# One pooled projection moved ahead of V, and products with V that move their operand in alternation

## The chip, the cores and the metric

The kernel runs on one core of a Trainium2 chip. A core has a matrix engine (TensorE, PE in the profile, with PEld for its weight loads), a vector engine (VectorE, DVE), a scalar engine (ScalarE, ACT), GpSimd (POOL) and a queue engine (SyncE, SP) that here issues most DMAs. Each has its own queue of instructions, which it works through in order; semaphores tie the queues together. Matrix products read SBUF and add into PSUM, which has eight banks of 128 partitions by 512 float32 values here.

The metric is the device time of one execution in microseconds (us), taken as the median of several runs.

## The reference

One layer of a streaming encoder over 512 tokens of width 1024, in float32: a half-weighted feed-forward, a mixer, a second half-weighted feed-forward, and a final norm.

```python
x = x + 0.5 * swiglu_ffn(rmsnorm(x, g1), w_gate1, w_up1, w_down1)
x = x + hybrid_mixer(rmsnorm(x, g), w_in, q_gain, k_gain, rel_bias, pool_w, pool_scale, w_out)
x = x + 0.5 * swiglu_ffn(rmsnorm(x, g2), w_gate2, w_up2, w_down2)
x = rmsnorm(x, g_final)
```

The mixer projects its input to q, k, v and u, each 512 wide. With q, k and v it computes chunked attention for 8 heads of 64 (each query sees its own chunk of 64 tokens and the 8 before it, with a relative-position bias; q and k are normed per head). With u it computes, in four groups of 128 channels, the trailing mean over 2, 4, 8 or 16 tokens less the token itself, then a 128 by 128 map and a scale. Both results are put side by side and go through one output projection.

```python
proj = h @ w_in                       # q | k | v | u
a = chunked_attention(q, k, v, ...)   # softmax(q k / 8 + bias) v, by head
p = multiscale_pool(u, pool_w, pool_scale)
return concat([a, p]) @ w_out
```

## The kernel before

**Precision by threes.** A float32 operand is split into a high part (rounded, made by ACT) and a low part (the remainder, made by DVE). A product is three matmuls: high with high, high with low, low with high. The function `mm3` writes them at lines 198 to 200, so three rows L198, L199, L200 are one "triple" over one block of 128 by 128 weights and 512 (sometimes 256) columns. `mm3` views the moving operand as two halves and moves a column of the first, then one of the second, in alternation; the result then stands in PSUM in that mixed order, and whoever takes it out reads PSUM with a stride of two (`ordered`) and writes in natural order (`natural`).

**Stages.** The first feed-forward, the mixer (about 310 to 496 us of the span) and the second feed-forward follow each other; only the mixer is changed.

**The mixer's order is planned.** Every piece of work is a `job` with an engine, a cost, a rank and the jobs that it waits for. `plan` walks through time with these costs, lets each engine take the ready job with the lowest rank for which there are buffers (eight PSUM banks, three places for split weights, two for raw weights and so on), and that sequence is written out for PE, DVE, ACT and POOL word for word. On the chip the engines keep to it, whatever the real durations are. Projections and the output projection are fillers: PE takes them when nothing of the attention is ready.

**The projections.** `ORDER` lists them: the query-key columns of heads 0 to 3 (`0`), V, the query-key columns of heads 4 to 7 (`1`), and the four pooled groups (`"u"`, the one with window 16 first). Each query-key half and V takes four weight blocks of 1024 columns, each pooled group takes one, that is 8 triples. SP loads raw blocks, ACT splits off the high part (L1117), DVE the low part (L1122). POOL also issues DMAs that add up weights for the second feed-forward (L717), tied to split blocks 12 to 19.

**A pooled group** after its projection: DVE scales it (L1422), POOL makes window sums (L1430, one to four steps), DVE forms the difference (L1438, and L1443 and L1444 for the first tokens), ACT and DVE split it (L1447, L1450), PE maps it (a triple that reads `wp`), ACT and DVE split the mapped result (L1263, L1267).

**A head**: scores (L1516, two heads at a time), bias and maximum on DVE (L1524), exponential on ACT (L1532), reciprocal (L1540), normalization on ACT (L1543), transposes on PE (L1580), the transposed probabilities split by ACT (L1589, high) and DVE (L1594, low) in three groups, then the product with V: eight matmuls at L1605, stationary the four blocks of V (with high and low side by side, so that one product gives two results of 64 rows), moving the probabilities' high and low parts. The keys are in four blocks of 128; block `j` moves only columns from `j * 128` on, so the eight are of 512, 512, 384, 384, 128, 128, 256 and 256 columns. ACT takes out the high half (L1612), DVE the rest (L1615) and the sum with the low half (L1621).

**The output projection** begins with the first four blocks of output rows, over the attention's heads 0 to 3, the pooled groups, and heads 4 to 7 in that order; the other blocks may begin after head 7's product.

Of the kernel before, what the change touches and what calls it, by code (L numbers as in the profile page):

```python
# [8 lines left out]
F32 = mybir.dt.float32  # L9
# [3 lines left out]
ALU = mybir.AluOpType  # L13
# [3 lines left out]
P = 128  # L17
# [3 lines left out]
NT = S // P  # L21
# [4 lines left out]
HD = 64  # L26
# [14 lines left out]
LATE = 12  # L41


ORDER = (0, "v", 1, "u", "u", "u", "u")
RANK = dict(
    weights=(-1.0, 0.905, 3.0), qk=2.0, turn=1.015, head=0.9, pool=0.965, map=3.0, u=0.99,
    score=0.99, evac=0.3, bias=1.2, wp=1.5, add=0.935, next=0.965,
# [9 lines left out]
def layer(  # L57
# [31 lines left out]
    nc = tc.nc  # L89
# [851 lines left out]
    with tc.tile_pool(name="mix", bufs=1, reuse_waits="tile") as mpool:  # L941
# [30 lines left out]
        def in_mix(tag, n, dtype, bufs, many=1):  # L972
            def make(slot):
                z = [
                    mpool.tile([P, n], dtype, tag=f"{tag}{i}", name=name(tag), bufs=bufs)
                    for i in range(many)
                ]
                return z if many > 1 else z[0]

            return bufs, make  # L980

        def part_at(slot):
# [10 lines left out]
            u=in_mix("u", PAD + S, F32, 1),  # L993
# [5 lines left out]
        buf = {}  # L999
# [84 lines left out]
        begins = []  # L1084
        for what in ORDER:
            begins.append(len(sources))
            if what == "v":
                sources += [wV[kp] for kp in KPS]
            elif what == "u":
                sources.append(wU[3 - sum(z == "u" for z in ORDER[: len(begins) - 1])])  # L1090
            else:
# [35 lines left out]
        for i in range(len(sources)):  # L1127
            z = job("sp", 0.4, i, load_raw(i), gets=[("raw", ("raw", i))], lag=2.0 if i < RAW else 3.6)
# [12 lines left out]
        for k, t in enumerate((7.2, 8.5, 9.7, 12.8)):  # L1141
            z = job("sp", 0.0, -9, None, lag=t)
# [46 lines left out]
        z = job("act", 1.8, -1, root_of, [z])  # L1189
        at_r = job("dve", 0.8, -1, reciprocal_root, [z], uses=["total"])  # L1190
        z = job("dve", 0.65, -1, diagonal, [at_r], [("t", "diag")])
        z = job("pe", 0.9, -1, spread, [z], [("bank", "wide")], ["diag"])
# [62 lines left out]
        z = job("sp", 0.4, 5, lambda: nc.sync.dma_start(buf["wp"], wP), gets=[("t", "wp")], lag=3.6)  # L1255
        z = job("act", 0.6, RANK["wp"], pool_weights(0), [z, ready[3]])
# [49 lines left out]
        v, at_v = [None] * NT, [None] * NT  # L1306
# [175 lines left out]
        n_u, n_before = 0, len(jobs)  # L1482
        for what, first in zip(ORDER, begins):
            if what == "u":
# [84 lines left out]
        def head(h):  # L1569
            rank = RANK["head"] + 0.01 * h - 0.001  # L1570
            rows = slice((h % 2) * HD, (h % 2 + 1) * HD)
            spots = {}
            pair = [("aT", h // 2, n) for n in range(2)]
# [14 lines left out]
            def high(group, n):  # L1588
                return lambda: nc.scalar.copy(buf["pT", h, group][0], buf["tp", h, group][:, :n])  # L1589
# [8 lines left out]
                return emit  # L1598

            def multiply():  # L1600
                o = buf["o", h]
                for j in (0, 1, 3, 2):
                    group, at = spots[j]
                    for i in range(2):
                        nc.tensor.matmul(  # L1605
                            o[:, j * P :], v[j][:, h, :, :],
                            buf["pT", h, group][i][:, at : at + (NT - j) * P],
                            start=j == 0 and i == 0, stop=j == 2 and i == 1,
                        )

            def out_high():
                nc.scalar.copy(buf[pair[0]][rows, :], buf["o", h][:HD, :])  # L1612

            def out_rest():
                nc.vector.tensor_tensor(  # L1615
                    buf["rest", h][rows, :], buf["o", h][:HD, :],
                    buf[pair[0]][rows, :].bitcast(F32), op=ALU.subtract,
                )

            def out_low():  # L1620
                nc.vector.tensor_tensor(  # L1621
                    buf[pair[1]][rows, :], buf["rest", h][rows, :], buf["o", h][HD:, :], op=ALU.add
                )

            lows = []
            for group in GROUPS:
                n = 0
                for j in group:
                    spots[j] = group, n
                    n += (NT - j) * P  # L1630
                z = at_turn[h, group] = job(
                    "pe", 0.03 + n / P * 0.109, rank, turned(group),
                    [at_prob[h, t] for t in range(min(group), NT)] + [at_turn.get((h - 1, group))],
                    [("bank", ("tp", h, group))], [("p", h, t) for t in range(min(group), NT)],
                )
                z = job(
                    "act", 0.13 + n * 0.00082, rank, high(group, n), [z],
                    [("wide" if n == S else "slim", ("pT", h, group))],
                )
                lows.append(  # L1640
                    job("dve", 0.08 + n * 0.00106, rank, low(group, n), [z], uses=[("tp", h, group)])
                )
            z = at_product[h] = job(
                "pe", 1.28, rank, multiply, lows + at_v, [("bank", ("o", h))],
                [("pT", h, group) for group in GROUPS],
            )
            z = job("act", 0.53, rank, out_high, [z], [("m", key) for key in pair])
            z = job("dve", 0.62, rank, out_rest, [z], [("t", ("rest", h))])
# [60 lines left out]
        for ds, chunks in (((0, 1, 2, 3), FOUR), ((4, 5), (0, 1)), ((6, 7), (0, 1))):  # L1709
            units = {d: [] for d in ds}  # L1710
            for chunk in chunks:
                if len(ds) == 4:
                    part, k0 = chunk
                    i = first_out + FOUR.index(chunk)
                    items = [(part, k, d) for k in ((k0, k0 + 1) if part else (k0 + 1, k0)) for d in ds]
                else:
                    part, k0 = chunk, 0
                    i = first_out + ds[0] + part
# [13 lines left out]
            for d in ds:  # L1732
                z = job("dve", 0.65, RANK["add"], add_out(d), units[d], uses=[("out", d)])
# [30 lines left out]
    with tc.tile_pool(name="act2", bufs=1, reuse_waits="tile") as apool, ExitStack() as in_order:  # L1764
# [86 lines left out]
        for tt in range(2):  # L1851
            scaled(u2[tt], p1[tt][0][0], 0.5, u2[tt], ALU.subtract)
            residual(1, 2 + tt, p5[tt][0][0])
            for i in (2 + tt, NT + tt, NT + 2 + tt):
                op = ALU.subtract if i < NT + 2 else ALU.add
                z = natural(xt[i])
# [45 lines left out]
        with tc.manual_schedule(engines={E.PE, E.DVE, E.Activation, E.Pool}):  # L1902
            last_product(0, p7[0][0])
            settle(0, two, 0, 0, S)
            v = mean(two, [1])
            r = inverse(v)
            v = small.tile([P, 1], F32, tag="rc", name=name("v"), bufs=8)
# [9 lines left out]
            v = more(v, 0)  # L1917
            root = small.tile([P, 1], F32, tag="rc", name=name("root"), bufs=8)
            nc.scalar.activation(root, ssq[:, three, 2:3], AF.Sqrt, scale=1.0 / D, bias=v)
            u = more(v, 2)  # L1920
# [94 lines left out]
```

## Time and profile before

| what | value |
|---|---|
| time, median of 3 runs | 811.85 us (811.62 to 812.27) |
| the profiled execution's own time | 811.69 us |
| its span, first to last instruction | 809.7 us |
| granted TensorE clock | 0.997 |
| PE busy | 797.8 us, 99% |
| DVE, ACT, POOL busy | 712.8, 498.8, 147.2 us |
| PE idle by its waits in the mixer | 0.6 us for L1621, 0.3 us for L1594 |

In the profile a row names the engine, the line of the program, the instruction and the tiles: `mm` and `a` are PSUM banks, `m` split parts, `parts` split weights, `pTw` and `pTs` transposed probabilities, `v` the blocks of V. PE's instructions are pipelined: a matmul's time reaches past the start of the next, so the pace is read from starts, not from durations.

### The profile page before, as it was taken

The page shows a single profiled execution, that of the slowest core. Times are in us where ns is not written, and L with a number is a line of the kernel's source. Part 1 is how long each engine was busy: PE and PEld are TensorE (multiplying, and loading weights), DVE is VectorE, ACT ScalarE, POOL GpSimd, SP SyncE. Part 2 cuts the span into 40 slices and gives each one's busy share as a digit, 9 for nine tenths or more (in the row PEclk, how much of TensorE's full clock was granted, in tenths as well). Part 3 has the DMA queues.
Part 4 walks back from the last instruction along what each step waited for, and adds up shares of the span by engine and source line. Part 5 has one row for each costly group of instructions (what it writes and reads, how often), then busy time and mean ns, then how long its engine had stood idle before and what let it go on. Part 6 is the DMA issues. An engine that isn't in the chain of part 4 may idle for free.

```text
span 809.7 us, 14959 instructions
## 1 busy us (share of the span) xinstructions
PE 797.8 (99%) x5730; PEld 749.1 (93%) x5730; DVE 712.8 (88%) x1133; ACT 498.8 (62%) x854; POOL 147.2 (18%) x234
## 2 busy tenths in 40 slices
PE   9999999999999999999999999999999999999995
PEld 8889999999999999888888888899999999988985
DVE  7899999999996997778688788999999999987996
ACT  8446655556666665659659545465666655765683
POOL 0022212223220000100256354111111011100010
PEclk9999999999999999999999999999999999999998
DMA  8276889979999774431599777256666566969642
GB/s 289 76 208 208 237 226 247 216 189 249 248 292 316 220 219 147 142 124 34 156 258 248 196 198 210 80 112 204 172 184 151 163 185 168 272 210 344 211 120 104
DMA packets 73703, 158.56 MB, mean 196 GB/s; under 512 B 6544, under 2 KB 31648, under 8 KB 73248
## 3 DMA queue, kind: packets, MB, share of 16 engines
q1 hardware_dynamic: 49664, 109.09, 40.0%
q0 software_dynamic: 23680, 48.24, 28.3%
q8 instruction: 45, 0.74, 0.4%
q10 hardware_dynamic: 288, 0.27, 0.1%
q14 instruction: 26, 0.21, 0.1%
HBM read 153.38 MB, written 50.34 MB: 252 GB/s over the span
## 4 chain that ended last, share of the span: by engine, by line
PE 91%; DVE 4%; ACT 1%; issue 1%; DVEq 0%; ACTq 0%
PE mm L198 19%; PE mm L200 19%; PE mm L199 19%; PE a L199 10%; PE a L200 9%; PE a L198 9%; PE mm L1605 1%; PE mm L1516 1%; DVE aside L365 1%; PE a L1580 1%; PE mm L1580 1%; DVE aside L371 0%; PE a L1516 0%; DVE parts L133 0%; PE a L1605 0%
## 5 line engine op out<-in xcount | busy, mean ns | idle before, releaser
L571 ACT ACTIVATE t<-mm 128x256 f32<-128x256 f32 x105 | 40.5, 386 | 110.8 <-PE mm L200 108.8
L132 ACT CAST parts<-raw 128x1024 fp32r<-128x1024 f32 (+2 forms) x77 | 74.1, 968 | 54.7 <-PE mm L199 20.5
L133 DVE TENSOR_TENSOR parts<-raw,parts 128x1024 fp32r<-128x1024 f32 (+2 forms) x77 | 85.8, 1121 | 15.1 <-ACT parts L132 14.7
L199 PE MATMUL mm<-ha,parts 128*128 128x256 f32 x280 | 77.0, 275 | 0.0
L200 PE MATMUL mm<-ha,parts 128*128 128x256 f32 x280 | 77.0, 275 | 0.0
L198 PE MATMUL mm<-ha,parts 128*128 128x256 f32 x280 | 77.0, 275 | 0.0
L715 POOL COPY mark<-t 128x1 f32<-128x1 f32 x40 | 15.9, 397 | 330.9 <-DVE t L615 244.8
L717 POOL DMA_DIRECT2D wsum<-in_wB_dram x72 | 71.1, 1123 | 26.1 <-DMA wsum<-wsum 14.1
L482 DVE TENSOR_TENSOR parts<-wsum,parts 128x1024 fp32r<-128x1024 f32 x53 | 64.5, 1217 | 5.1 <-ACT parts L477 5.1
L477 ACT CAST parts<-wsum 128x1024 fp32r<-128x1024 f32 x53 | 53.9, 1047 | 0.6 <-PE mm L200 0.3
L198 PEld LDWEIGHTS mm<-ha,parts 128*128 128x128 f32 x280 | 53.8, 192 | 0.1
L199 PEld LDWEIGHTS mm<-ha,parts 128*128 128x128 f32 x280 | 53.8, 192 | 0.1
L200 PEld LDWEIGHTS mm<-ha,parts 128*128 128x128 f32 x280 | 53.8, 192 | 0.0
L198 PE MATMUL mm<-hhi,parts 128*128 128x512 f32 x128 | 49.6, 391 | 0.2
L200 PE MATMUL mm<-hhi,parts 128*128 128x512 f32 x128 | 48.7, 384 | 0.8 <-DVE parts L133 0.8
L133 DVE TENSOR_TENSOR ah<-acts,ah 128x512 fp32r<-128x512 f32 (+1 forms) x72 | 47.1, 662 | 2.7 <-ACT ah L132 2.4
L199 PE MATMUL mm<-hlo,parts 128*128 128x512 f32 x128 | 48.4, 379 | 0.0
L132 ACT CAST ah<-acts 128x512 fp32r<-128x512 f32 (+1 forms) x72 | 40.9, 580 | 8.8 <-PE mm L199 6.4
L482 DVE TENSOR_TENSOR parts<-raw,parts 128x512 fp32r<-128x512 f32 (+1 forms) x52 | 43.6, 858 | 0.5 <-ACT parts L477 0.5
L500 DVE TENSOR_TENSOR wsum<-raw 128x1024 f32<-128x1024 f32 x35 | 42.6, 1217 | 0.0
L477 ACT CAST parts<-raw 128x512 fp32r<-128x512 f32 (+1 forms) x52 | 39.2, 755 | 4.7 <-DMA raw<-in_wA_dram 3.4
L1122 DVE TENSOR_TENSOR parts<-raw,parts 128x1024 fp32r<-128x1024 f32 x24 | 30.1, 1258 | 11.6 <-ACT parts L1117 11.5
(342 smaller groups left out, 3062.0 us busy)
## 6 DMA issues: line engine op xcount, KB each, us to landing
raw<-in_wA_dram SPq DMA_DIRECT2D x87, 512.0 KB, 4.7
wsum<-in_wB_dram POOLq DMA_DIRECT2D x60, 512.0 KB, 7.5
raw<-wsum SPq DMA_DIRECT2D x36, 512.0 KB, 4.6
raw<-in_wB_dram SPq DMA_DIRECT2D x30, 512.0 KB, 4.9
wsum<-wsum POOLq DMA_DIRECT2D x20, 512.0 KB, 5.0
x<-in_xT_dram SPq DMA_DIRECT2D x16, 256.0 KB, 6.1
raw<-in_wQK_dram SPq DMA_DIRECT2D x8, 512.0 KB, 3.6
wsum<-in_wB_dram POOLq DMA_DIRECT2D x12, 256.0 KB, 5.5
```

What stands on the lines that cost most here:

```text
L132: nc.scalar.copy(hi, src)
L133: nc.vector.tensor_tensor(lo, src, hi.bitcast(F32), op=ALU.subtract)
L198: nc.tensor.matmul(acc, a[0], high, start=start, stop=False, **more)
L199: nc.tensor.matmul(acc, a[0], low, start=False, stop=False, **more)
L200: nc.tensor.matmul(acc, a[1], high, start=False, stop=stop, **more)
L477: nc.scalar.copy(hi, src)
L482: nc.vector.tensor_tensor(lo, src, hi.bitcast(F32), op=ALU.subtract)
L500: nc.vector.tensor_tensor(z, raw[:, : 2 * S], raw[:, S : 3 * S], op=ALU.add)
L571: nc.scalar.activation(natural(dst), ordered(src), AF.Copy, scale=scale)
L717: nc.gpsimd.dma_start(self.rows(i, g), self.rows(self.terms[i][at], g), **(dict(accum_op=ALU.add) if at else {}),)
L1122: nc.vector.tensor_tensor(lo, buf["raw", i], hi.bitcast(F32), op=ALU.subtract)
L1580: nc.tensor.transpose(buf["tp", h, group][:, n : n + P], buf["p", h, t][:, j * P : (j + 1) * P], ident,)
```

## The change

Two things, both in the mixer.

```diff
-ORDER = (0, "v", 1, "u", "u", "u", "u")
+ORDER = (0, "u", "v", 1, "u", "u", "u")
@@ head: products with V
             def multiply():
-                o = buf["o", h]
+                o = buf["o", h].rearrange("p (b i a) -> p b i a", a=2, i=P // 2)
                 for j in (0, 1, 3, 2):
                     group, at = spots[j]
                     for i in range(2):
+                        turned = buf["pT", h, group][i][:, at : at + (NT - j) * P]
                         nc.tensor.matmul(
-                            o[:, j * P :], v[j][:, h, :, :],
-                            buf["pT", h, group][i][:, at : at + (NT - j) * P],
+                            o[:, j:], v[j][:, h, :, :],
+                            turned.rearrange("p (b a i) -> p b i a", a=2, i=P // 2),
                             start=j == 0 and i == 0, stop=j == 2 and i == 1,
                         )
 
+            def result(half):
+                o = buf["o", h][half * HD : (half + 1) * HD, :]
+                return o.rearrange("p (b i a) -> p b a i", a=2, i=P // 2)
+
+            def by_block(z):
+                return z[rows, :].rearrange("p (b a i) -> p b a i", a=2, i=P // 2)
+
             def out_high():
-                nc.scalar.copy(buf[pair[0]][rows, :], buf["o", h][:HD, :])
+                nc.scalar.copy(by_block(buf[pair[0]]), result(0))
```

`out_rest` and `out_low` change their operands in the same way.

**The order.** The pooled group with window 16 is projected between the first query-key half and V. It is no more than an entry moved in a tuple, but the planner makes a new sequence for the whole mixer out of it.

**The alternation.** Within each block of 128 columns the products with V now move a column of the first 64 and one of the second 64 in turn. The result stands in that order in its bank, and the three instructions that take it out read it with a stride of two and write natural order. The number of instructions and their sizes are the same.

Lines after the change are 1 to 8 higher from there on: the product is L1606, its evacuation L1620, L1623 and L1629.

On PE, at the end of the first query-key half (`mm_4306` is its last bank), before:

```order
L200 MATMUL mm_4306<-parts,hlo_4256 128x512
L198 MATMUL a_4469<-parts,hhi_4121 128x512
L199 MATMUL a_4469<-parts,hhi_4121 128x512
L200 MATMUL a_4469<-parts,hlo_4122 128x512
L198 MATMUL a_4475<-parts,hhi_4121 128x512
```

and now:

```order
L200 MATMUL mm_4306<-parts,hlo_4256 128x512
L198 MATMUL a_4469<-hhi_4234,parts 128x512
L199 MATMUL a_4469<-hlo_4235,parts 128x512
L200 MATMUL a_4469<-hhi_4234,parts 128x512
L198 MATMUL a_4469<-hhi_4241,parts 128x512
```

Behind the arrow the moving operand stands first. Where V's triples began (they move the split weights past the tokens, in four banks), the pooled group's eight triples stand now (they move the tokens past the split weights, all into one bank), and V's follow.

On PE, ahead of head 6's product (its bank is `a_5717` before and `mm_5764` after), before:

```order
L198 MATMUL mm_5683<-m_5604,wp_4378 128x512
L199 MATMUL mm_5683<-m_5605,wp_4378 128x512
L200 MATMUL mm_5683<-m_5604,wp_4379 128x512
L198 MATMUL mm_5697<-m_5611,wp_4378 128x512
L199 MATMUL mm_5697<-m_5612,wp_4378 128x512
L200 MATMUL mm_5697<-m_5611,wp_4379 128x512
L1580 MATMUL a_5705<-ident,prob_804_5510 128x128
L1580 MATMUL a_5705<-ident,prob_799_5486 128x128
L1605 MATMUL a_5717<-pTw_5691,v_4748 128x512
```

and now:

```order
L198 MATMUL a_5752<-m_5711,wp_4378 128x512
L199 MATMUL a_5752<-m_5712,wp_4378 128x512
L200 MATMUL a_5752<-m_5711,wp_4379 128x512
L198 MATMUL a_5665<-m_5674,parts 128x512
L199 MATMUL a_5665<-m_5675,parts 128x512
L200 MATMUL a_5665<-m_5674,parts 128x512
L1606 MATMUL mm_5764<-pTw_5727,v_4827 128x512
L1606 MATMUL mm_5764<-pTw_5728,v_4827 128x512
```

Two maps and a pair of transposes for head 7 stood right ahead of it; now one map and a triple of the output projection stand there, and between the products of heads 5 and 6 there are seven triples where there were three.

On ACT, the last instructions ahead of head 7's probability copies (L1589 into `pTw`), before:

```order
L1543 ACTIVATE prob_809_5538<-prob_809_5538,sm_5487 128x256
L1117 CAST parts<-raw_5345 128x1024
L1612 CAST m_5735<-a_5717 64x512
L1447 CAST m_5742<-t_5709 128x512
L1589 CAST pTw_5750<-mm_5730 128x512
```

and now:

```order
L1117 CAST parts<-raw_5533 128x1024
L1620 CAST m_5790<-mm_5764 64x512
L1589 CAST pTs_5797<-mm_5784 128x256
L1543 ACTIVATE prob_825_5594<-prob_825_5594,sm_5546 128x128
L1543 ACTIVATE prob_826_5598<-prob_826_5598,sm_5546 128x256
L1117 CAST parts<-raw_5656 128x1024
L228 ACT_TABLE_LOAD
L228 ACTIVATE table<-ones 128x1
L1589 CAST pTw_5841<-a_5822 128x512
```

Two normalizations of head 7 (L1543), a second weight split and the table load now stand between head 6's result and these copies, where a pooled difference (L1447) stood.

More of the change, by code (lines that the diff above doesn't have):

```diff
@@ L1604, in multiply @@
                     for i in range(2):
+                        turned = buf["pT", h, group][i][:, at : at + (NT - j) * P]
                         nc.tensor.matmul(
-                            o[:, j * P :], v[j][:, h, :, :],
-                            buf["pT", h, group][i][:, at : at + (NT - j) * P],
+                            o[:, j:], v[j][:, h, :, :],
+                            turned.rearrange("p (b a i) -> p b i a", a=2, i=P // 2),
                             start=j == 0 and i == 0, stop=j == 2 and i == 1,
                         )
+            def result(half):
[3 more added lines that the diff above has]
+                return z[rows, :].rearrange("p (b a i) -> p b a i", a=2, i=P // 2)
             def out_high():
-                nc.scalar.copy(buf[pair[0]][rows, :], buf["o", h][:HD, :])
+                nc.scalar.copy(by_block(buf[pair[0]]), result(0))
             def out_rest():
                 nc.vector.tensor_tensor(
-                    buf["rest", h][rows, :], buf["o", h][:HD, :],
-                    buf[pair[0]][rows, :].bitcast(F32), op=ALU.subtract,
+                    by_block(buf["rest", h]), result(0), by_block(buf[pair[0]].bitcast(F32)),
+                    op=ALU.subtract,
                 )
@@ L1621, in out_low @@
                 nc.vector.tensor_tensor(
-                    buf[pair[1]][rows, :], buf["rest", h][rows, :], buf["o", h][HD:, :], op=ALU.add
+                    by_block(buf[pair[1]]), by_block(buf["rest", h]), result(1), op=ALU.add
                 )
```

## The prediction

> **What bounds the kernel now.** I read the page's engine totals and its chain first, then the stretch of the mixer in which the change works.
>
> ```profile
> PE 797.8 (99%) x5730; PEld 749.1 (93%) x5730; DVE 712.8 (88%) x1133; ACT 498.8 (62%) x854; POOL 147.2 (18%) x234
> PE 91%; DVE 4%; ACT 1%; issue 1%; DVEq 0%; ACTq 0%
> ```
>
> TensorE is busy for 99% of the span, and the chain that ended last runs over PE for 91%. So what counts is the time that PE spends per matmul and the few places where it waits. The totals hide the second, so I asked for the busy time from the second half's scores to head 4's product with V, and from there to head 7's (columns: window, PE, weight loads, DVE, ACT, POOL, clock, DMA share, GB/s).
>
> ```profile
> 420.00:433.30 13.30, 13.30 (x95) 11.32 (x95) 12.10 (x47) 11.09 (x34) 11.66 (x14) 1.00 0.99 249
> 433.30:454.40 21.10, 20.09 (x110) 16.93 (x109) 20.02 (x45) 20.23 (x43) 9.95 (x14) 1.00 0.71 176
> ```
>
> The clock is full (1.00). In the second stretch DVE (20.02 of 21.10 us) and ACT (20.23) are as full as PE, and only there does PE stop. Its timeline (start, time, instruction, wait in brackets):
>
> ```profile
> 443.06 0.60 PE L1580 MATMUL a<-ident,prob 128*128 128x128 f32 x4
> 443.72 0.45 PE L198 MATMUL mm<-m,wp 128*128 128x512 f32 x1
> 444.23 0.38 PE L200 MATMUL mm<-m,wp 128*128 128x512 f32 x1
> 445.17 0.45 PE L198 MATMUL mm<-m,wp 128*128 128x512 f32 x1 [0.56 <-DVE m L1621]
> 445.97 0.44 PE L1580 MATMUL a<-ident,prob 128*128 128x128 f32 x2
> 446.73 1.27 PE L1605 MATMUL a<-pTw,v 128*128 128x512 f32 x6 [0.32 <-DVE pTw L1594]
> ```
>
> Starts should follow each other by 0.22 us after a 512-wide matmul and 0.11 per transpose. 443.06 to 443.72 is 0.66 where 0.44 is due (0.2 lost), 444.23 to 445.17 is 0.94 for 0.22 (0.7), 445.97 to 446.73 is 0.76 for 0.27 (0.5); with 0.1 at head 6's first matmul and 0.2 behind its last, **PE loses about 1.8 us here**. The chain of waits says to whom:
>
> ```profile
> 443.61 0.69 DVE t L1615
> 444.32 0.69 DVE m L1621
> 445.47 0.60 DVE m L1450
> 446.07 0.61 DVE pTw L1594
> ```
>
> DVE works without a gap through head 5's result (L1615, L1621), a pooled difference (L1450) and head 6's probabilities (L1594), and PE waits for its queue.
>
> **The change, part by part.** *Alternating moves.* The projections' matmuls already move two halves of their operand alternately; the products with V move straight ahead. Their pace side by side, around head 0's product:
>
> ```profile
> 378.71 0.38 PE L199 MATMUL mm<-parts,hhi 128*128 128x512 f32 x1
> 379.57 0.38 PE L200 MATMUL mm<-parts,hlo 128*128 128x512 f32 x1
> 379.79 1.15 PE L1605 MATMUL mm<-pTw,v 128*128 128x512 f32 x6
> 380.78 0.45 PE L1605 MATMUL mm<-pTs,v 128*128 128x256 f32 x2
> 381.07 0.38 PE L198 MATMUL a<-parts,hhi 128*128 128x512 f32 x1
> ```
>
> Five alternating 512-wide matmuls take 379.79 - 378.71 = 1.08 us, 0.216 each (0.42 ns a column). The eight of a product take 381.07 - 379.79 = 1.28 us. The same eight at the alternating pace: two of 512 at 0.216, two of 384 at 0.162, and four of 128 and 256 columns at 0.109, the pace of narrow alternating matmuls in the feed-forward:
>
> ```profile
> 129.95 0.28 PE L200 MATMUL a<-xa,wlo 128*128 128x256 f32 x1
> 130.50 0.28 PE L199 MATMUL mm<-xa,parts 128*128 128x256 f32 x1
> ```
>
> That is five starts in 0.55 us. The sum is 0.43 + 0.32 + 0.44 = 1.19, so 0.09 less per head and **-0.7 us** for eight heads, all of it on PE. What no row shows is an alternation over 64 columns (256 bytes); the rows have 256 and 128 columns. Bounds: nothing gained, and the full 0.7. I take the full value, since both distances in the trace run at the same pace. A loss is priced under the rivals.
>
> The Trainium skill ("TensorE: Matmul & The Clock Gate", back-to-back issue gap) gives a matmul N/2.4 + 2.5 ns whatever its addresses, 215.8 ns for 512; by it the sum here would be zero. The 1.28 us above stand against it, since its figures would give an estimated 1.09 for the product already now.
>
> *The results of the product.* They now leave PSUM with a stride of two. ACT and DVE pay nothing measurable for that:
>
> ```profile
> L1612 ACT CAST m<-mm x6: 577/578/580, 381.3 to 455.9; 64x512 fp32r<-64x512 f32 x6
> L1312 ACT ACTIVATE t<-mm,r x6: 687/687/688, 342.3 to 405.4; 128x512 f32<-128x512 f32 x6
> L1422 DVE TENSOR_TENSOR u<-mm,rb x2: 671/678/684, 434.2 to 442.9; 128x512 f32<-128x512 f32 x2
> ```
>
> L1422 reads with that stride in 678 ns, where the straight L1615 takes 0.69 us. ACT's strided, scaled L1312 takes 687 ns against 578, at most 0.11 more. I count nothing; without cover it would be 0.1 us on each of two or three heads whose result PE waits for.
>
> *The pooled projection.* Its 24 matmuls keep their time, and so do its weight split, window sums and map: moved, not added. Its weight load passes the four V loads and four query-key loads on SP; on POOL its four window sums go ahead of the weight-sum DMAs instead of between them. Up to the first scores PE has 26 triples (three 512-wide matmuls, 0.65 us) where it had 25, and 28 instead of 17 between the first scores and head 0's product, so the first half gets 7 us more cover for some 4 us of extra ACT and DVE work. I count no wait there.
>
> The scores now fall into eight groups instead of seven. Entering and leaving one costs PE time:
>
> ```profile
> 419.73 0.38 PE L200 MATMUL mm<-hhi,parts 128*128 128x512 f32 x1
> 420.04 0.49 PE L1516 MATMUL mm<-m,m 64*128 64x512 f32 x1
> 420.38 0.39 PE L1516 MATMUL mm<-m,m 64*128 64x512 f32 x1
> 422.17 0.48 PE L198 MATMUL mm<-hhi,parts 128*128 128x512 f32 x1
> 422.49 0.38 PE L199 MATMUL mm<-hlo,parts 128*128 128x512 f32 x1
> ```
>
> 0.31, 0.34 and 0.32 where 0.22 is the pace: **+0.3 us**.
>
> *The late stretch.* Between the products of heads 4 and 7 PE has 25 triples instead of 19, with the same 28 transposes: 21.1 - 1.8 + 3.9 - 0.3 = 22.9 us of its own work. DVE loses one pooled difference with its edge (1.0 like the other pooled steps together), two L1450 (1.2) and one L1422 (0.6), and gains a map's low part (0.7, as L1615) and a weight split (1.2, below): about 19 us. So DVE is no longer the bound, and between heads 5 and 6 stand seven triples instead of three. **The old 1.8 us go.** But ACT gains there, priced by:
>
> ```profile
> L1117 ACT CAST parts<-raw 128x1024 fp32r<-128x1024 f32 x24 | 25.1, 1047 | 19.0 <-PE mm L200 9.2 <-PE a L199 5.8 <-DMA raw<-in_wQK_dram 2.2
> L1532 ACT ACTIVATE prob<-prob,sm 128x512 f32<-128x512 f32 (+3 forms) x32 | 17.7, 556 | 5.0 <-DVE sm L1524 4.9
> L1543 ACT ACTIVATE prob<-prob,sm 128x512 f32<-128x512 f32 (+3 forms) x32 | 16.9, 559 | 0.0
> L228 ACT ACT_TABLE_LOAD x3 | 3.8, 1283 | 0.1
> L1447 ACT CAST m<-t 128x512 fp32r<-128x512 f32 x4 | 2.4, 630 | 0.0
> L1122 DVE TENSOR_TENSOR parts<-raw,parts 128x1024 fp32r<-128x1024 f32 x24 | 30.1, 1258 | 11.6 <-ACT parts L1117 11.5
> ```
>
> One weight split (1.05), one map (0.6), one normalization (0.5) and the table load with its dummy (1.5), less two L1447 (1.1), all a little under their means since neighbours overlap: +2.5 us, about 22 of 22.9. It is full, and unevenly so. From head 6's last probability copy to head 7's last normalization it has twelve instructions: four normalizations, three exponentials, two maps, a weight split, a head's result, a copy: 4 x 0.5 + 1.5 + 2 x 0.6 + 1.0 + 0.5 + 0.35 = 6.5 us, starting about 1 us before head 6's product. PE reaches the transposes for which it needs them after 1.2 + 5 x 0.65 + 0.3 = 4.8 us. **A new wait of about 0.7 us** stands there. Ahead of head 4's product the cover shrinks. Its last operand and its start were:
>
> ```profile
> 431.17 0.68 DVE L1594 TENSOR_TENSOR pTw<-a,pTw 128x512 fp32r<-128x512 f32 x1
> 433.14 1.14 PE L1605 MATMUL a<-pTw,v 128*128 128x512 f32 x6
> ```
>
> That is 433.14 - 431.85 = 1.3 us of slack. Now PE has 9 triples instead of 11 there (1.3 less) while DVE gets a split and an L1450 more and a pooled difference less. The slack is used up, and I put 0.3 there and at head 5. Together +1.0, bounds 0 and 2.5 (both waits at twice the size and the ones of before in part).
>
> **Sum** against the profiled execution's 811.69 us: -0.7 + 0.3 - 1.8 + 1.0 = -1.2, 810.5. The median of the runs is 811.85, 0.16 above the profiled one, so **810.6 us**.
>
> **The rivals.** *The old wait goes and no new one comes* (ACT has its normalizations done in time): -0.7 + 0.3 - 1.8 + 0.2 = -2.0, 809.8. For it: in the stretch ahead ACT had 11.09 of 13.30 us, so it may start earlier. Against it: 22 of 22.9 us.
>
> *Alternation over 64 columns brings nothing*: 811.3.
>
> *The weights come late.* DMA is at 0.99 in the stretch before, and ACT's two splits of output weights now stand ahead of head 7's copies, with everything behind them in one queue. The slowest of such loads:
>
> ```profile
> DMA to landing us min/median/max: 3.3/3.6/7.8
> ```
>
> 4.2 us late, less ACT's 1 us of reserve, puts 3.2 on PE in place of the 0.7: 810.6 + 2.5 = 813.1. It decides once a load lands more than 1 us behind the split's turn.
>
> *Alternation costs.* If two addresses 256 bytes apart disturbed each other, the nearest slow pace is that of the unrounded 512-wide matmuls:
>
> ```profile
> 342.09 1.02 PE L1182 MATMUL a<-t,ones 128*128 128x512 f32 x2
> L1182 PE MATMUL a<-t,ones x2: 593/593/593, 342.1 to 342.5; 128*128 128x512 f32 x2
> ```
>
> 1.02 - 0.593 = 0.43 us apart, twice 0.216. A product of 2560 columns would take 2.14 instead of 1.28 us: +6.9 for eight heads in place of -0.7, 818. It decides the sign once a product costs 0.06 us more than now, which eats the 0.5 us gained elsewhere. The Trainium skill ("SBUF — State Buffer", Door 1: The DMA port swizzle) says that reads that cross to a new 16-byte line each time pay a penalty, which speaks for this; the alternating triples, faster than the straight products, speak against it.
>
> **How the numbers follow.** Forecast 0.45 (810.0 to 811.1), no new wait 0.22, no gain from alternation 0.20, late weights 0.07, costly alternation 0.06. A change under 0.2% (1.6 us, 810.2 to 813.5) can't be told from none. The forecast lies just inside: of its 0.45 I give 0.13 to faster, of the second case 0.21; late weights divide 0.04 slower, 0.03 same. So faster 0.34, same 0.56, slower 0.10. The range leaves out a tenth at each end: 809.3 to 812.4.
>
> **What would show it.** Eight products of 1.19 us, and eight evacuations still near 0.58 us; PE starting its maps on time between heads 5 and 6; a wait of PE for ACT's L1543 ahead of head 7's transposes; at most 0.5 us lost at head 4. Products of 1.28 us would make the first term wrong; waits in the first half or a PE wait behind a weight split would make the others wrong.

## The result and the profile after

The changed kernel takes 819.02 us (median of 6 runs, 816.74 to 821.42) where the kernel before, run beside it, takes 811.94: a ratio of 1.0086 (95% interval 1.0068 to 1.0103). It is slower by 7 us. I had forecast 810.6, in a range that ended at 812.4.

The profiled execution after took 819.33 us, 7.6 more than the one before. First the chain that ended last, from its page:

```profile
PE 81%; DVE 6%; DMA 4%; ACT 2%; issue 2%; POOL 1%; SPq 0%; DVEq 0%; ACTq 0%; POOLq 0%
```

The chain, which ran over PE for 91%, now runs over it for 81% and over DMA for 4%. PE's waits of 0.3 us and more (which line waited for what; us in total, times, longest), without three outside the mixer that the kernel before has too:

```profile
PE a L1516 <- ACT m L1447: 4.8, 1, 4.8
PE mm L1356 <- DVE t L1346: 1.1, 1, 1.1
...
PE a L198 <- ACT t L571: 0.7, 1, 0.7
...
PE a L198 <- DVE m L1629: 0.3, 1, 0.3
```

The first two are new in the mixer. One score group of the second half (L1516) waits 4.8 us, and the transposes of the first query-key half (L1356) wait 1.1 us. L571 lies in the first feed-forward, which the change does not touch. The wait for L1629 stands at 452.8 us, behind head 4's result (452.22 to 452.91 us on VectorE); the wait for head 5's result that I had read in the kernel before is gone.

The chain of waits through the long one, in order of time (start, us, what):

```profile
411.63 8.66 DMA wsum<-in_wB_dram
...
422.76 1.73 POOL wsum L717 x2
424.49 5.91 issue
...
430.95 1.09 POOL us L1430
...
433.25 1.06 POOL us L1430
...
434.34 0.69 DVE t L1438
...
435.35 0.63 ACT m L1447
436.07 0.76 PE a L1516
```

GpSimd issues two weight-sum DMAs (L717). The third of the same step reads a sum that another DMA is still making, so it can be issued only 5.91 us later, as GpSimd's timeline shows as well (start, time, instruction, wait in brackets):

```profile
430.42 0.53 POOL L717 DMA_DIRECT2D wsum<-wsum  x1 [5.93 <-DMA wsum<-in_wB_dram]
```

Behind it in GpSimd's queue stand the window sums (L1430) of the second pooled group, window 8. They end at 434.3 us. VectorE's L1438 waits for them, and ScalarE's L1447 waits for that. VectorE's timeline says what this holds up:

```profile
434.34 0.69 DVE L1438 SCALAR_TENSOR_TENSOR t<-us,u 128x512 f32<-128x512 f32 x1 [6.46 <-POOL us L1430]
...
435.23 0.69 DVE L1524 CUSTOM_DVE_ANT_0 prob<-a,bias 128x512 f32<-128x512 f32 x1
```

and ScalarE's:

```profile
435.35 0.62 ACT L1447 CAST m<-t 128x512 fp32r<-128x512 f32 x1 [7.55 <-DVE t L1444]
435.96 0.72 ACT L1532 ACTIVATE prob<-prob,sm 128x512 f32<-128x512 f32 x1
```

VectorE stands still for 6.46 us and ScalarE for 7.55, each in front of a pooled step, while the score maxima (L1524) and exponentials (L1532) of the third pair of heads stand right behind it. Without the pooled step in front, the first L1524 starts at 429.66 us (experiment 4). PE needs the bank that the first L1524 frees. The waits view names L1447 because its end lies next to PE's start.

Then the clock. The windows around the wait (columns: window, PE, weight loads, DVE, ACT, POOL, granted clock, DMA share, GB/s):

```profile
432.00:434.00 2.00, 0.00 (x0) 0.00 (x0) 0.00 (x0) 0.00 (x0) 1.84 (x3) 0.88 1.26 491
...
438.00:440.00 2.00, 2.00 (x14) 1.88 (x11) 1.84 (x11) 2.00 (x8) 0.00 (x0) 0.50 0.98 172
440.00:442.00 2.00, 2.00 (x12) 1.39 (x12) 1.58 (x10) 1.97 (x6) 0.00 (x0) 0.92 1.08 188
```

In the middle of the stretch the mean is 0.50. If the clock is either full or half, a mean of 0.88 puts the drop at 433.5 us (1.52 us in full and 0.48 by half), 0.92 puts the return at 440.3. (Windows of half a microsecond bear this out: 1.00 up to 433.5, then 0.51 and 0.50, and 0.67 from 440.0 to 440.5 before 1.00.) PE works again from 436.07, so 4.2 us of work ran at half speed, which costs 2.1 us.

The alternation does what it says. Head 0's product on PE's timeline after:

```profile
390.46 1.09 PE L1606 MATMUL mm<-pTw,v 128*128 128x512 f32 x6
391.66 0.38 PE L198 MATMUL a<-parts,hhi 128*128 128x512 f32 x1
```

That is 391.66 - 390.46 = 1.20 us, where it was 1.28.

**The balance** of the two profiled executions: +4.8 (wait) + 2.1 (half clock) + 1.1 (L1356) + 0.3 (the eighth score group, taken from the prediction, not measured by itself) - 0.7 (alternation) - 1.8 (the old late wait) + 0.3 (the wait for L1629) + 1.4 (the mixer starts later, see experiment 9) = 7.5 of 7.6 us.

### The profile page after: what moved, and what is told of

Read it like the earlier page. It is cut to its first block, busy times and chain, and to the rows that moved or that the text cites. A ratio compares the mean times of both kernels' runs of the same rounds, so it can differ in the third digit from the quotient of the medians.

```text
span 817.5 us, 14948 instructions
## 1 busy us (share of the span) xinstructions
PE 799.9 (98%) x5730; PEld 750.7 (92%) x5730; DVE 716.3 (88%) x1133; ACT 499.3 (61%) x854; POOL 148.2 (18%) x234
## 4 chain that ended last, share of the span: by engine, by line
PE 81%; DVE 6%; DMA 4%; ACT 2%; issue 2%; POOL 1%; SPq 0%; DVEq 0%; ACTq 0%; POOLq 0%
PE mm L198 18%; PE mm L200 18%; PE mm L199 18%; PE a L198 8%; PE a L199 8%; PE a L200 8%; DMA wsum<-in_wB_dram 3%; DMA raw<-in_wA_dram 1%; PE mm L1516 1%; DVE t L1346 1%; DVE aside L365 1%; POOL wsum L717 1%; PE mm L1606 0%; DVE aside L371 0%; POOL us L1430 0%
## 5 line engine op out<-in xcount | busy, mean ns | idle before, releaser
L571 ACT ACTIVATE t<-mm 128x256 f32<-128x256 f32 x105 | 40.5, 386 | 110.6 <-PE mm L200 108.3
L717 POOL DMA_DIRECT2D wsum<-in_wB_dram x72 | 71.9, 1153 | 29.5 <-DMA wsum<-wsum 15.8
L1122 DVE TENSOR_TENSOR parts<-raw,parts 128x1024 fp32r<-128x1024 f32 x24 | 31.2, 1299 | 9.7 <-ACT parts L1117 9.7
```

The source lines that it names most:

```text
L571: nc.scalar.activation(natural(dst), ordered(src), AF.Copy, scale=scale)
L717: nc.gpsimd.dma_start(self.rows(i, g), self.rows(self.terms[i][at], g), **(dict(accum_op=ALU.add) if at else {}),)
L1122: nc.vector.tensor_tensor(lo, buf["raw", i], hi.bitcast(F32), op=ALU.subtract)
```

## The experiments

Each kernel was run beside the kernel before on the same chip, whose median was 812.0 to 812.2 us.

**1 and 2. Each half of the change alone.** The first is the changed kernel with the old `ORDER`, so that the alternation stays:

```diff
-ORDER = (0, "u", "v", 1, "u", "u", "u")
+ORDER = (0, "v", 1, "u", "u", "u", "u")
```

> The alternation of the column halves alone, in the order of the kernel before. Theory (the loss belongs to the moved projection): the eight products keep the 1.20 us that the trace after the change shows instead of 1.28, so 0.7 us are gained and the time is 811.2 us, ratio 0.9991, with no new wait on TensorE over 0.5 us in the mixer. Rival (the alternation loses elsewhere, through the evacuations that read and write in strides): part of the 7 us comes with it, 813 us or more.

Measured: 811.42 us against 812.12, ratio 0.9992 (0.9983 to 1.0000). PE's waits in the mixer are those of the kernel before:

```profile
PE mm L198 <- DVE m L1629: 0.6, 1, 0.6
...
PE a L1606 <- DVE pTw L1594: 0.3, 1, 0.3
```

The second kernel is the one before with the new `ORDER` and straight products.

> The moved projection alone, with the products' columns in their old order. Theory: the whole loss is here. The 4.8 us wait at the scores of the second half stands in the trace at about 431 to 436 us, and the time is that of the changed kernel plus the 0.7 us that the alternation gave: 819.7 us, ratio 1.0095. Rival (the strided evacuations hold up VectorE and ScalarE and the order only brings it to light): the wait is gone or under 1 us, and the time is 813 us or less.

Measured: 818.43 us, ratio 1.0077 (1.0063 to 1.0091). The long wait is there, though shorter than expected:

```profile
PE a L1516 <- ACT m L1447: 3.0, 1, 3.0
```

Its windows, with the end of the lowered clock:

```profile
438.00:440.00 2.00, 2.00 (x9) 1.38 (x9) 0.78 (x4) 1.06 (x4) 0.00 (x0) 0.50 1.03 187
440.00:442.00 2.00, 2.00 (x11) 1.65 (x10) 1.99 (x5) 1.07 (x5) 1.47 (x1) 0.92 0.57 104
```

So the order brings the loss, +6.3, and the alternation, -0.7, is no part of it. I had expected 819.7, and the two do not quite add up to the 7.1 of the whole change: 5.6, within the width of the intervals, with a long wait that took 3.0 us in this profile and 4.8 and 4.0 in the two of the changed kernel. The wait is 1.8 us shorter than in the changed kernel, but the time hardly is, because the clock is at half from 433.5 (432 to 434 us has a mean of 0.87) to 440.3 us here too, and all but 0.05 us of that is work: 3.4 us lost instead of 2.1.

**3. The weight-sum DMAs behind the window sums.** The list is written out with one step of GpSimd moved (position 398 in the planned list) behind the second group's sums (411):

```diff
-            for z, got in plan():
+            planned, behind = plan(), {398: 411}
+            held = {}
+            for n, (z, got) in enumerate(planned):
                 ...
-                if z.emit:
-                    z.emit()
+                if n in behind:
+                    held.setdefault(behind[n], []).append(z)
+                    continue
+                for y in (z, *held.pop(n, [])):
+                    if y.emit:
+                        y.emit()
                 ...
```

> The changed kernel, with one step of GpSimd's queue moved: the three weight-sum DMAs that stood just ahead of the second pooled group's window sums (window 8) are issued behind these sums. Theory (the sums come late because they queue behind a DMA whose issue waits for other DMAs to land): the sums end about 6 us earlier, near 428 us, the 4.8 us wait of TensorE at 431 us is under 0.7 us, the clock granted from 430 to 440 us is over 0.95, and the time falls by 6.5 to 7 us to about 812.3 us. Rival A (the scores wait for ScalarE's evacuations or for the keys, not for GpSimd): the wait stays above 3 us and the time at 819 us. Rival B (the wait goes, but the lowered clock has another cause): about 814.3 us, with the granted clock still under 0.8 from 430 to 440 us.

Measured: 811.82 us, ratio 0.9994 (0.9985 to 1.0004): 7 us are back. GpSimd's timeline and VectorE's:

```profile
420.56 2.86 POOL L1430 TENSOR_TENSOR us<-us 128x525 f32<-128x525 f32 x2
...
427.81 0.69 DVE L1438 SCALAR_TENSOR_TENSOR t<-us,u 128x512 f32<-128x512 f32 x1
```

PE's waits of the mixer but for one of 0.2 us:

```profile
PE mm L1356 <- DVE t L1346: 2.2, 2, 1.2
```

and the window of the old wait:

```profile
430.00:440.00 10.00, 10.00 (x70) 8.16 (x67) 9.80 (x39) 9.96 (x29) 5.23 (x8) 1.00 1.06 285
```

The sums end at 423.4 us, earlier than the 428 that I expected, VectorE takes L1438 without a wait, and PE is busy for the whole of 430 to 440 us at full clock. That names the cause: the loss is the place of the sums in GpSimd's queue, behind a DMA that is issued late. Rival A falls. Rival B falls too: no wait, no lowered clock. What I had not expected is a second L1356 wait, in the second half (2.2 us for two where there was one of 1.1).

**4. Let the sums be late, and move only those that wait for them.** The same device with other positions (the lines are against experiment 3): L1438 with its edge steps, L1447, L1450 and the map's product stand behind the third pair's scores.

```diff
-            planned, behind = plan(), {398: 411}
+            planned, behind = plan(), {431: 463, 434: 466, 465: 470, 473: 495}
```

> The changed kernel with GpSimd's queue as it is: the window sums end as late as before, near 434 us. Only what waits for them is moved in its queue: VectorE's L1438 with its two edge steps and its L1450, and ScalarE's L1447, stand some 15 instructions later, behind the score maxima and exponentials of the third pair, and the map's product two output products later. Theory (what costs is not that the sums are late but that VectorE and ScalarE stand still in front of them while ready work is queued behind): the 4.8 us wait is under 0.7 us and the time is 812 to 813 us, as when the sums are moved. Rival (the late sums themselves, or the DMA traffic of these microseconds, hold up TensorE): the wait stays above 3 us or moves to the map's product, and the time stays over 816 us.

Measured: 814.11 us (812.68 to 817.03), ratio 1.0027 (1.0013 to 1.0040). The sums run to 432.6 us, a little earlier than I expected, and VectorE no longer stands in front of them. GpSimd's timeline, and VectorE's:

```profile
430.39 2.20 POOL L1430 TENSOR_TENSOR us<-us 128x525 f32<-128x525 f32 x2
```

```profile
429.66 0.69 DVE L1524 CUSTOM_DVE_ANT_0 prob<-a,bias 128x512 f32<-128x512 f32 x1 [1.46 <-PE a L1516]
```

PE's 4.8 us wait is gone with sums that end 3 us after the first maximum began. So the theory holds for the wait, but the time is 2.3 us above experiment 3, where I had expected no difference. I ran it again (experiment 10).

**5. Why L1346 is slow.** Of the first group's four adding passes on GpSimd three are left out:

```diff
-                while step < win:
+                while step < (2 if win == 16 else win):
```

> The changed kernel, with the window sums of the first pooled group (window 16) cut from four adding passes on GpSimd to one; three passes are left out, so this group's values are wrong. Theory (VectorE's instructions whose operands all lie in SBUF take turns with GpSimd's adds: the last three L1346 took 1.55 us each beside the adds, the first 0.68 us without): only one L1346 keeps about 1.5 us, the other three take 0.68 us, the 1.1 us wait of TensorE at L1356 is under 0.3 us, the first transposes to the first scores take 4.4 to 4.6 us instead of 5.68, and the time falls by 1.1 to 1.3 us to about 817.8 us. The 4.8 us wait in the second half stays. Rival (the wait comes from L1422, which now stands ahead of the four L1346): the wait stays at 0.7 us or more, and the time above 818.5 us.

Measured: 817.38 us, ratio 1.0069 (1.0047 to 1.0090), 1.6 us below the changed kernel. That difference says little, since the long wait and the clock behind it came out differently too; the first half says more. From the first transposes (L1356) to the first scores PE takes 4.4 us here and in the kernel before, 5.7 after the change. VectorE's four L1346 (they scale the queries and keys) on the timeline of the kernel before:

```profile
352.91 2.49 DVE L1346 TENSOR_TENSOR t<-t,z 128x512 f32<-128x512 f32 x4
```

after the change:

```profile
354.88 5.08 DVE L1346 TENSOR_TENSOR t<-t,z 128x512 f32<-128x512 f32 x4
```

and with one adding pass:

```profile
353.68 3.36 DVE L1346 TENSOR_TENSOR t<-t,z 128x512 f32<-128x512 f32 x4
```

GpSimd's last three adds beside them, after the change:

```profile
356.56 4.53 POOL L1430 TENSOR_TENSOR us<-us 128x525 f32<-128x525 f32 x3
```

Four add passes cost the four L1346 2.6 us, one pass costs 0.9. The L1356 wait is gone although L1422 still stands ahead, so the rival falls. VectorE and GpSimd take turns here (the last section has the times): an L1346 reads two tiles of SBUF, an L1430 too.

The long wait was 2.9 us in this profile, yet the half clock lasted longer, about 10.2 us by its windows (a drop at 431.0, a return at 441.3; those between show 0.50):

```profile
430.00:432.00 2.00, 0.28 (x1) 0.28 (x1) 1.97 (x6) 1.56 (x3) 2.00 (x5) 0.76 0.42 122
...
440.00:442.00 2.00, 2.00 (x9) 1.59 (x9) 0.82 (x5) 1.19 (x5) 1.92 (x2) 0.68 0.21 53
```

**6. Both causes removed, by place alone.** Nothing is left out: the first two groups' evacuations (L1422) stand behind the four L1346 and the L1122 that follows, so the adds run beside VectorE's L1267. The lines are again against experiment 3:

```diff
-            planned, behind = plan(), {398: 411}
+            planned, behind = plan(), {118: 129, 122: 129, 136: 138, 145: 155, 150: 159, 158: 160, 397: 408, 398: 411, 416: 418, 431: 440, 434: 446}
```

> The changed kernel with both pooled groups moved some places in the queues: the evacuation L1422 of the first two groups stands behind the four L1346 and the L1122 after them, so that GpSimd's adds run while VectorE evacuates from PSUM (L1267); the weight-sum DMAs ahead of the second group's adds stand behind them; L1438 and L1447 stand a few instructions later. Theory (two costs, turns with GpSimd at L1346 and still queues in front of late sums): both L1356 waits, 1.1 us in the first half and 1.2 us that came in the second half when the sums were moved ahead of the DMAs, fall under 0.4 us together, the 4.8 us wait is gone, and the time is 809.2 to 810.2 us, ratio about 0.997. Rival (the adds slow VectorE whatever it does): L1267 takes 1.3 us or more instead of 0.75 beside the adds, the scores come late by 1 us or more in each half, and the time stays at 811.5 us or more.

Measured: 810.87 us against 812.21, ratio 0.9985 (0.9976 to 0.9993), faster than the kernel before, though 0.7 us above the upper end of what I had expected. Against the alternation alone (0.9992) the intervals overlap. The eight L1346 of both halves (min/median/max ns), in experiment 3:

```profile
L1346 DVE TENSOR_TENSOR t<-t,z x8: 681/1542/1558, 353.5 to 422.4; 128x512 f32<-128x512 f32 x8
```

and here:

```profile
L1346 DVE TENSOR_TENSOR t<-t,z x8: 682/685/687, 353.3 to 419.3; 128x512 f32<-128x512 f32 x8
```

Of PE's waits in the mixer one is left:

```profile
PE a L1516 <- DVE sm L1524: 0.3, 1, 0.3
```

The adds lie beside L1267, and neither is slowed where they meet (GpSimd's timeline and VectorE's):

```profile
358.85 3.56 POOL L1430 TENSOR_TENSOR us<-us 128x525 f32<-128x525 f32 x3
358.96 2.07 DVE L1267 SCALAR_TENSOR_TENSOR m<-mm,qk_sb,m 128x512 fp32r<-128x512 f32 x3 [1.41 <-ACT m L1263]
```

Three L1267 in 2.07 us is 0.66 from start to start, as in the kernel before beside no add (358.57 to 359.89 us there), and three adds take 3.56 us instead of 4.53; only the last of them, which outlasts the L1267, takes more than 1.06 us. L1267 reads one of its tiles from PSUM. The rival, that adds slow VectorE whatever it does, falls.

**7. Tell the planner.** The step of DMAs counted at 8.0 us instead of 3.8:

```diff
-                "pool", 3.8, 5, lambda i=i: down2.make_sums(...),
+                "pool", 8.0, 5, lambda i=i: down2.make_sums(...),
```

> The changed kernel with one number of the planner changed: a step of weight-sum DMAs on GpSimd is counted at 8.0 us instead of 3.8. The list then has the second group's window sums ahead of the DMA step by itself, and all later work is planned around it. Theory: the 4.8 us wait at the scores of the second half is under 0.7 us and the time is 811 to 812.5 us, as with the step moved by hand; a wait of about 1 us at L1356 in the first half stays, since the first group's adds stay where they are. Rival (the wait has moved to another place because DMAs now land late for the second feed-forward block): over 814 us.

Measured: 815.65 us, ratio 1.0040 (1.0026 to 1.0053). A miss. The plan puts the sums ahead by itself and the long wait is gone, but all the rest is planned anew, and the last heads' products meet other waits:

```profile
PE mm L1606 <- ACT pTw L1589: 1.0, 1, 1.0
...
PE mm L1606 <- DVE pTs L1594: 0.6, 1, 0.6
```

The clock drops behind them:

```profile
466.00:468.00 2.00, 1.37 (x8) 1.18 (x7) 1.18 (x3) 0.08 (x1) 0.00 (x0) 0.78 0.10 39
...
470.00:472.00 2.00, 2.00 (x10) 1.72 (x9) 0.00 (x0) 0.00 (x0) 0.00 (x0) 0.87 0.04 8
```

With 0.50 in between, that is half the clock from 467.1 to 470.5 us, although no single wait there was longer than about 1.0 us.

The time is the rival's, the mechanism is not: no late DMA, but ScalarE's and VectorE's copies for the products (ScalarE's stands behind a table load of 1.28 us). A truer cost in one place did not make a better list.

**8. The alternation at half the distance.**

```diff
-o = buf["o", h].rearrange("p (b i a) -> p b i a", a=2, i=P // 2)
+o = buf["o", h].rearrange("p (b i a) -> p b i a", a=2, i=P // 4)
```

The moving operand and the results are viewed in the same way.

> The alternation alone, in the order of the kernel before, with pieces half as wide: columns 32 apart alternate instead of 64 apart. Theory (any two pieces that lie apart will do): the four 512-column moves of a product keep a pitch of 216 ns and the time is 811.4 us, that of the alternation alone. Rival (the gain needs pieces that lie 64 columns or more apart): the pitches go back to 230 ns or more and the time to 812.1 us.

Measured: 811.23 us against 812.21, ratio 0.9987 (0.9978 to 0.9997). The 512-column moves stay 216 ns apart in the trace. Columns 32 apart do as well as 64.

**9. The change again.**

> The changed kernel once more, beside runs of the kernel before on the same chip. In its first profile the stretch from TensorE's first matmul to the first L1151, which the change does not touch, took 336.32 us; in the profiles of the kernel before and of six experiments it took 334.7 to 335.4. One raw weight tile (in_wA) had landed 1.9 us late for L477 at 206.7 us. Theory (a landing that now and then comes late, in any kernel): this profile shows 334.7 to 335.4 us, and the time is 817.5 to 819 us. Rival (it belongs to this build of the program): again 336.0 us or more, and 819 us or more. In both, the wait at 431 us is there again, of 3 to 5 us.

Measured: 819.67 us, ratio 1.0092 (1.0066 to 1.0118), with a wait of 4.0 us. When the mixer begins is seen from its first matmuls (L1151; the times are the first and the last start), in the kernel before:

```profile
L1151 PE MATMUL a<-ones,acc x8: 167/250/250, 336.0 to 336.7; 128*128 128x1 f32 x8
```

in the first profile of the change:

```profile
L1151 PE MATMUL a<-ones,acc x8: 167/250/250, 337.4 to 338.1; 128*128 128x1 f32 x8
```

and in this one:

```profile
L1151 PE MATMUL a<-ones,acc x8: 167/250/250, 336.5 to 337.2; 128*128 128x1 f32 x8
```

Of the 1.4 us by which the first profile began late 0.9 are gone with the same program, so the most of it varies from run to run and is no part of the change. I had expected a lower time for it, 817.5 to 819, and that did not come: here PE waited 4.0 us, and the half clock (434.8 to 441.6 by its windows) fell wholly on work, 3.4 us, so wait and clock cost 7.4 us instead of 6.9.

**10. The moved queues again.**

> The kernel with VectorE's and ScalarE's waiting instructions moved past the scores once more; its profile had 336.65 us up to the first L1151, and its times lay between 812.7 and 817.0 us. Theory (late landings in the first block and luck of the runs): 334.7 to 335.4 us here and a time near 812.5 us, that of the kernel with the sums moved ahead. Rival (the sums are still late enough in some executions to hold up what now stands behind them): up to the first L1151 it takes 335 us, but the median stays at 813.5 us or more, and the mixer's own stretch, 155.4 us from the first L1182 to the second block's start in the first profile, is 157 us or more where the time is high.

Measured: 814.65 us (813.32 to 817.39), ratio 1.0031 (1.0018 to 1.0044), with the mixer beginning at 336.0 us. So the 2 to 3 us above experiment 3 are real, and a late first block is not their cause. The mixer's own stretch is 157.6 us, the rival's number, where 155.4 was. All of the difference lies between the first scores of the second half and head 4's product (16.3 us here, 14.0 in experiment 4's profile): ScalarE stands at a weight split that is queued ahead of the exponentials, and waits for its raw weights.

```profile
430.19 1.05 ACT L1117 CAST parts<-raw 128x1024 fp32r<-128x1024 f32 x1 [4.76 <-DMA raw<-in_wO_dram]
431.14 0.72 ACT L1532 ACTIVATE prob<-prob,sm 128x512 f32<-128x512 f32 x1
```

In experiment 4's profile the same split began at 427.06 us without such a wait. It is one more instruction in front of ready work that waits for a DMA, this time ScalarE's. That the DMAs of these microseconds land now earlier and now later is shown by the two profiles; that it makes up all of the difference in the medians is not.

## Why the prediction was wrong, point by point

**What bounded the kernel**: right. PE at 99%, and the wait of 1.8 us behind a full VectorE at heads 5 to 7. After the change it is gone.

**The alternation, -0.7**: right in mechanism and size. 1.20 us a product (1.19 predicted), -0.7 us alone. The results that leave PSUM in strides cost nothing, as ScalarE's group after says (min/median/max ns; L1612 before had 577/578/580; VectorE's L1623 keeps the median of 684 ns that L1615 had):

```profile
L1620 ACT CAST m<-mm x4: 577/578/579, 391.9 to 472.1; 64x512 fp32r<-64x512 f32 x4
```

The rivals "brings nothing" and "costs" are out, the first by the length of the products: the interval of the medians alone (0.9983 to 1.0000) would just let it stand.

**The eighth score group, +0.3**: not measured by itself; the balance leaves room for it.

**"… on POOL its four window sums go ahead of the weight-sum DMAs instead of between them … I count no wait there": this step failed.** It followed the moved group only, and the sum has no term for GpSimd's queue in the second half, where the 4.8 us of wait and the 2.1 us of clock behind it came. The planner had made a new list for the whole mixer, in which the next group's sums came to stand behind a weight-sum step and its L1438 and L1447 ahead of the third pair's maxima and exponentials. The prediction asked what the moved group passes on GpSimd's queue, and not what now stands behind which DMA in the second half. The size of such a wait stood in the trace of before. GpSimd's timeline there, and VectorE's:

```profile
415.52 0.50 POOL L717 DMA_DIRECT2D wsum<-wsum  x1 [6.48 <-DMA wsum<-in_wB_dram]
```

```profile
421.49 0.68 DVE L1524 CUSTOM_DVE_ANT_0 prob<-mm,bias 128x512 f32<-128x512 f32 x1
...
425.57 0.68 DVE L1438 SCALAR_TENSOR_TENSOR t<-us,u 128x512 f32<-128x512 f32 x1
```

GpSimd stood for 6.48 us in front of a DMA there too. It cost nothing, since L1438 came at 425.57, 4 us behind the first score maximum of that half. With those rows and the order of VectorE's new list, a wait of several us could have been priced as a rival.

**Clock**: I had no term for it. "The clock is full (1.00)" was true of a kernel whose waits were short. A wait of 3 to 5 us cost its own length and, in the four profiles that have one, 2 to 5 us more.

**"I count no wait" in the first half**: wrong by 1.1 us. I had counted PE's cover and not VectorE's pace. That VectorE's instructions on two SBUF tiles slow down beside GpSimd's adds was in the trace of before as well, where VectorE's timeline has an L1122 beside three L1430 (418.29 to 422.71 us on GpSimd's):

```profile
419.63 1.93 DVE L1122 TENSOR_TENSOR parts<-raw,parts 128x1024 fp32r<-128x1024 f32 x1
```

Elsewhere it takes 1.22 us. The Trainium skill ("SBUF — State Buffer", Who interferes with whom) states it: a VectorE instruction with two inputs in SBUF contends with a GpSimd instruction that reads SBUF, and one of them waits for the whole of the other; with at most one input in SBUF, outside the modes in which VectorE uses two ports, it does not. The runs agree, with 1.55 against 0.68 us for L1346 and 0.66 us a start for L1267 either way.

**"The old 1.8 us go"**: right. From head 4's product to head 7's PE takes 22.9 us in experiments 4, 6 and 10, the own work that I had counted, and 23.4 in the changed kernel.

**"A new wait of about 0.7 us" at head 7's transposes and 0.3 at heads 4 and 5**: the first did not come. Experiment 6, in which the second half runs without the long wait, has none there either, so the waiting is not merely hidden. ScalarE's twelve instructions take 7.0 us, near the 6.5 of the sum, but they begin 3.6 us before head 6's product (457.62 against 461.26 us in the changed kernel) and not 1, and end 1.3 us before the transposes that need them. Of the other 0.3 the changed kernel has the wait for L1629, right in size by luck: it stands behind head 4's product, not ahead of it, and is not the late operand that the prediction counted.

**The rival "weights come late", 813.1**, had the right kind of cause, an engine that stands in front of a DMA with a full queue behind it, but the wrong queue, place and price: GpSimd's sums instead of raw weights, and nearly 7 us instead of 2.5. Experiment 10 saw the raw weights' form of it.

## What to carry to other kernels

When one moved entry makes a planner write a new list, look at every instruction that waits for a queue with DMAs in it, and ask what stands behind it on its own engine: ready work behind a late operand costs the whole lateness, whatever the engine's share of busy time. Count a PE wait of about 3 us, or several that add up to 2 us within a few microseconds, at more than its length: behind each wait of 2.9 us or more in these profiles, and behind one run of short ones, the clock was lowered. Lay GpSimd's adds beside vector work that reads PSUM, and check each DMA-issuing step of a planned queue against how long it really stands there.

## What the runs showed of the hardware

**The half clock comes in steps.** By the windows it lasted 3.4 us in experiment 7 (467.1 to 470.5), 6.8 in the changed kernel (433.5 to 440.3), in its repeat (434.8 to 441.6) and with the order alone (433.5 to 440.3), and 10.2 with one adding pass (431.0 to 441.3). These are one, two and three times 3.4 us. The longest waits were 1.0, 4.8, 4.0, 3.0 and 2.9 us in this order, so the length of the wait does not set the number of steps, and what does stays open. In the 3.4 us ahead of the drop PE stood idle for 1.7 us in experiment 7, 2.2 in the changed kernel and with one adding pass, and 3.0 in the other two. The Trainium skill ("TensorE: Matmul & The Clock Gate", What's actually happening) has a gate with two values, half and full, that goes by activity in free-running windows of about 3.4 us. The runs agree, and they add that half of such a stretch idle can be enough. It is not always: in experiment 10 PE stood idle for 1.8 of the 3.4 us from 436.4 on, and the clock stayed full (1.00).

**Turns, not shares.** Beside GpSimd's adds, L1346 starts came 1.46 to 1.48 us apart in the changed kernel's trace and those of the adds 1.45 to 1.47, one for one, where alone they follow each other at 0.60 and 1.14 us (experiment 6). Each of the three slow L1346 ends 0.55 or 0.56 us after the add in whose time it began (357.04 after 356.48, 358.50 after 357.95, 359.97 after 359.41 us), so it does its work when that add is done.

**Alternation.** Columns 32 and 64 apart in alternation move at 216 ns for 512, straight ones at 226 to 240 over the eight heads of the kernel before (in both forms without the first matmul of two or three products, which takes 0.30 us or more); why straight moves are slower no run here shows.
